# A hybrid encoder on one Trainium2 core: k's first four heads are turned by VectorE and DRAM instead of TensorE, and the opening and the layer border are put in another order

## The chip, the cores and the metric

The program runs on one core of one Trainium2 chip. The metric is the device time of one execution in microseconds (us). It is given as the median of the runs shown, and it stands beside one execution that was taken with a profile. The core has TensorE (PE in the profile, with its weight loads as PEld), VectorE (DVE), ScalarE (ACT), GpSimd (POOL) and SyncE (SP), which here issues transfers alone. Each engine takes its instructions in the order in which they stand in its own queue, and an instruction that waits holds up what stands behind it on that engine.

## The reference

Two layers (DEPTH = 2) over 256 tokens of width 1024, all in float32. A layer normalises its input, projects it by one wide matrix, runs two token mixers beside each other, gates and merges them and adds the result to its input. Cut to what matters here:

```python
for l in range(DEPTH):
    h = rmsnorm(x, norm_w[l])
    (q_a, k_a, v_a, ab_a, z_a, q_b, k_b, v_b, z_b, gate_a, gate_b) = split(h @ w_in[l])
    y_a = gated_delta_branch(q_a, k_a, v_a, ab_a, z_a, ...)   # short conv, silu, l2norm of q and k,
                                                              # chunked delta rule in both directions, 8 heads of 128
    y_b = diff_attention_branch(q_b, k_b, v_b, z_b, cos, sin, ...)   # partial rotary from positions
    merged = sigmoid(gate_a) * (y_a @ w_pa[l]) + sigmoid(gate_b) * (y_b @ w_pb[l])
    x = x + merged @ w_out[l]
return rmsnorm(x, final_norm_w)
```

For k the first branch needs both layouts: channels on the partitions (for the products of keys with keys and queries) and tokens on the partitions (`ktm`, for the update of the state), and the sum of squares of every token and head (`ssk`).

## The kernel before

**Products.** A float32 product is made of three products in a rounded format: each operand is split into a high part (ACT copies it into the rounded format) and a low part (DVE subtracts the high part from the original), and PE adds high by high, high by low and low by high. So every 512 KB piece of a weight matrix costs one transfer on SP's queue, one ACT cast (L290), one DVE subtraction (L292) and then the products. A weight matrix of 1024 rows and 512 columns comes in four such pieces, `kp` 0 to 3, each for two of the eight row blocks `kt`. The normalised input is turned by PE (`split_T`, L213) and split in the same way into `hT`, one half of it for `kt` 0 to 3 and one for 4 to 7, in two tiles `m` of 128 tokens.

**Order.** The scheduler of the language orders each engine's queue by a simulated time line and by priorities. The kernel's author steers it: `behind(ins)` puts an instruction after another in its engine's queue, and `mark` keeps the instructions that serve as such anchors.

**The opening.** The first norm's weights are one row. `norm_row` spreads it over the partitions: it lays the row into a tile of zeros and multiplies it by a matrix of ones below the diagonal, in two float32 products (L168). The positions come as one number per partition, in one small transfer on POOL's queue (L126). `prenorm` squares a token tile on ACT (L193), adds the sums on DVE (L188), takes the power on POOL (L189), multiplies on DVE (L203), and turns and splits both halves (L213, L219, L220). The first projection is v of the attention branch (`vb`, `proj_by_tile`, L364): it does all eight `kt` of token tile 0 and then all of token tile 1. Its first weight piece comes in halves (L276, L279, L281). Token tile 1 is loaded after weight piece 1, and its norm is made in the middle of tile 0's products. Later come `abp` (L563, sixteen small products) and then k.

**k, q and v of the first branch.** `proj_fm` leaves channels on the partitions. `evac_conv` then makes a head's short convolution: ACT scales (L610), DVE adds four taps (L614), ACT takes tanh (L620), DVE multiplies (L625). For k, `kq` holds the result, and for every pair of heads PE turns four blocks of 128 by 128 (L641) into a PSUM bank, ACT copies the bank to `ktm` (L643) and squares four blocks for `ssk` (L647). For v another way is in use already: DVE turns 32 by 32 blocks (`turn_squares`, L136), `bounce` writes them to DRAM (L141) and reads them back in four strided transfers (L143), all on POOL's queue, and `place_v` copies them on ACT later (L661). `log_decays` needs `ssk` of all heads, and the decays, `dsum` and `A` of the next stage hang on it.

**The border.** At the end of layer 0 the output projection's second half (`proj_by_tile`) is done tile by tile. After each tile its residual is added (L1207) and `prenorm` of the next layer runs, while `vb` of layer 1 begins with token tile 0. The turning of tile 1's first half stands ahead of the products of `kt` 6 of token tile 0.

Of the kernel before, what the change touches and what calls it, by code (L numbers as in the profile page):

```python
# [17 lines left out]
P = 128  # L18
# [31 lines left out]
def hybrid_encoder(  # L50
# [131 lines left out]
    def norm_factor(xt_, m, h, r, ss, halves_, after=None):  # L182


        for i in halves_:
            with behind(after):
                sq = mark["square", m, i] = square(xt_, m, h, ss, i)
        mark["sum"] = V.tensor_scalar(r, ss[:, 0:1], ss[:, 1:2], EPS, ALU.add, ALU.add).ins  # L188
        mark["pow"] = G.tensor_tensor(r, r, mhalf[:, :1], ALU.pow).ins  # L189
        return sq  # L190
# [4 lines left out]

    def normed(xt_, wb, m, nm, after=(None, None)):

        h, r, ss = norm_tiles(nm, m)
        sq = norm_factor(xt_, m, h, r, ss, range(2), after[0])
        for i in range(2):  # L200
            cs = slice(512 * i, 512 * i + 512)
            with behind(after[1]):
                hh = V.scalar_tensor_tensor(h[:, cs], xt_[i][:, m, :], r, wb[i],  # L203
                                            ALU.mult, ALU.mult).ins
        mark["norm", m] = sq, hh
        return h

    def split_T(dst, src, m, nm, bank=bank, w=None):


        pt = bank(f"pt_{nm}{m}")
        for j in range(4):
            tr = T.transpose(pt[:, j * P : (j + 1) * P], src[:, j, :], ident).ins  # L213
        mark["turn"] = tr
        ptv = pt.rearrange("p (j t) -> p j t", j=4)
        hi = dst[:, 0, :, m * P : (m + 1) * P]
        lo = dst[:, 1, :, m * P : (m + 1) * P]
        if w is None:
            a_ = S.copy(hi, ptv).ins  # L219
            mark["split"] = a_, V.tensor_tensor(lo, ptv, hi.bitcast(F32), ALU.subtract).ins  # L220
# [30 lines left out]
    def weights(w, c0, n, nm, homes=(None,) * 4, ahead=True, later=None, spare=(), held=None, turned=(), first=(),  # L251
                raws={}, halved={}):

# [3 lines left out]
        for kp in range(4):  # L257
            act, dve = (later or {}).get(kp, (None, None))
            act = mark[nm, act][0] if isinstance(act, int) else act
            with tc.high_priority(offset=HP) if ahead and (homes[kp] is None or kp in first) else nullcontext():  # L260
# [12 lines left out]
                if kp in halved:  # L273
                    for k in range(2):
                        rows = slice((2 * kp + k) * P, (2 * kp + k + 1) * P)
                        nc.sync.dma_start(out=raw[:, k, :n], in_=w[rows, c0 : c0 + n])  # L276
                        act, dve = halved[kp][k]
                        with behind(act):
                            high = S.copy(hi[:, k, :n], raw[:, k, :n]).ins  # L279
                        with behind(dve):  # L280
                            mark[nm, kp] = high, V.tensor_tensor(lo[:, k, :n], raw[:, k, :n],  # L281
                                                                 hi[:, k, :n].bitcast(F32), ALU.subtract).ins
                        yield 2 * kp + k, hi[:, k, :n], lo[:, k, :n]
# [38 lines left out]

    def proj_by_tile(act, w, c0, evac, nm, places, later=None, turn=None, spare=(), held=None, between=None,
                     cut=(), halved={}):

        accs = banks2(f"pp_{nm}")
        ws = []
        parts = weights(w, c0, 512, nm, places, ahead=False, later=later, spare=spare, held=held, halved=halved)  # L330
        if between is None:
            ws.extend(parts)
        for m in range(NM):
# [16 lines left out]
            for kt in range(KT):  # L350
                if len(ws) == kt:
                    if between and kt % 2 == 0:
                        between(kt)
                    ws.append(next(parts))
                if kt == 6 and turn and turn(m):
                    mark["proj"] = turn(m)
                if between and not m:
                    terms = [(kt - 1, 0, 0), (kt - 1, 1, 0), (kt, 0, 0), (kt, 1, 0),
                             (kt - 1, 0, 1), (kt, 0, 1)] if kt % 2 else []
                else:  # L360
                    terms = [(kt, 0, 0), (kt, 0, 1), (kt, 1, 0)]
                for n_, (k_, pa, pw) in enumerate(terms):
                    with behind(mark.get("proj")):
                        mark["proj"] = T.matmul(o, act[k_ // 4][:, pa, k_ % 4, ts_], ws[k_][1 + pw],  # L364
                                                start=k_ == 0 and n_ == 0,
                                                stop=kt == KT - 1 and n_ == len(terms) - 1).ins
            evac(m, o)
# [51 lines left out]
    def prenorm(m, xt_, wb_, l_, after=(None, None)):  # L419
        h = normed(xt_, wb_, m, f"n{l_}", after)  # L420
        for i in range(2):
            split_T(hT[i], heads4(h[:, 512 * i : 512 * i + 512]), m, f"h{l_}{i}", bank_c)
            mark["turn", m, i], mark["split", m, i] = mark["turn"], mark["split"]

    hT = pair("hT0")
    prenorm(0, xt, wb, 0)


    for l in range(DEPTH):
# [6 lines left out]
        def evac_v(i):  # L436
            def evac(m, ps):
# [8 lines left out]
                   for t_ in places2] + [places.pop(), *homes((("vtm", 1),), f"vb{l}1")]  # L446
        later, between, held, halved = {}, None, {}, {}
        if l == 0:
            halved[0] = (None, mark["norm", 0][1]), mark["split", 0, 0]

            def between(kt):
                if kt == 2:
                    later[1] = mark["split", 0, 1]
                elif kt == 4:
                    tokens(1)
                    prenorm(1, xt, wb, 0, mark["vb00", 1])
                    later[2] = mark["norm", 1]
                    mark["later"] = {0: mark["split", 1, 1]}
# [4 lines left out]
        for _ in proj_by_tile(hT, wl, C_VB, evac_v(0), f"vb{l}0", places, later=later,  # L463
                              spare=(1, 3) if l else (3,), held=held, halved=halved, between=between,
                              turn=lambda m: None if m or not l else mark["turn", 1, 0]):
            pass
        if l == 0:
# [3 lines left out]
            pos_f = const.tile([P, NM], F32, name="pos_f")  # L471
            with tc.issue_after(mark["split", 1, 1][1]):
                V.tensor_copy(pos_f, pos_i)
            freq = const.tile([P, RD], F32, name="freq")
# [128 lines left out]
        def conv(seg, c_base, slot, g):  # L603
            def evac_conv(acc, b0):
                vf = []
                for b in range(2):
# [12 lines left out]
                    th = ths[:, b, :]  # L619
                    S.activation(th, ca, AF.Tanh, scale=0.5)  # L620
                    if slot is None:
                        f_ = th.rearrange("p (m t) -> p m t", m=NM)
                    else:
                        f_ = kq[:, 4 * g + j4, :, slot, :]
                    mark["conv"] = V.scalar_tensor_tensor(  # L625
                        f_, th.rearrange("p (m t) -> p m t", m=NM), 1.0,
                        ca.rearrange("p (m t) -> p m t", m=NM), ALU.add, ALU.mult).ins
# [23 lines left out]

        loose = []

        def place_v(after):
# [633 lines left out]
```

## Time and profile before

| what | value |
|---|---|
| median of 3 runs | 751.92 us (751.69 to 752.0) |
| the profiled execution | 753.24 us, of which the profile's span is 751.5 us |
| granted TensorE clock in it | 0.997 |
| PE busy | 740.4 us |
| DVE busy | 588.9 us |
| ACT busy | 474.7 us |
| POOL busy | 143.1 us |
| bytes moved | 135.44 MB, mean 180 GB/s |

How to read it: the profiled execution is one run of its own and is 1.32 us longer than the median. A row of a time line gives start, duration, engine, source line, operation, output and inputs, and in square brackets how long the engine had been idle and what ended that. PE's matmuls are pipelined, so a matmul's duration is longer than its share of PE's time; the distance of two starts is the better price.

### The profile page before, as it was taken

The page shows a single profiled execution, that of the slowest core. Times are in us where ns is not written, and L with a number is a line of the kernel's source. Part 1 is how long each engine was busy: PE and PEld are TensorE (multiplying, and loading weights), DVE is VectorE, ACT ScalarE, POOL GpSimd, SP SyncE. Part 2 cuts the span into 40 slices and gives each one's busy share as a digit, 9 for nine tenths or more (in the row PEclk, how much of TensorE's full clock was granted, in tenths as well). Part 3 has the DMA queues.
Part 4 walks back from the last instruction along what each step waited for, and adds up shares of the span by engine and source line. Part 5 has one row for each costly group of instructions (what it writes and reads, how often), then busy time and mean ns, then how long its engine had stood idle before and what let it go on. Part 6 is the DMA issues. An engine that isn't in the chain of part 4 may idle for free.

```text
span 751.5 us, 13864 instructions
## 1 busy us (share of the span) xinstructions
PE 740.4 (99%) x5160; PEld 638.9 (85%) x5160; DVE 588.9 (78%) x1106; ACT 474.7 (63%) x1015; POOL 143.1 (19%) x221
## 2 busy tenths in 40 slices
PE   8999999999999999999999999999999999999996
PEld 5999889987888889888889889889778888998885
DVE  7786899999986865478667779999998769537782
ACT  6657665667877476645545577555777757566452
POOL 5100441111022440000010025202110425301000
PEclk9999999999999999999999999999999999999998
DMA  8752667776668462567674358768656847335641
GB/s 262 224 178 82 209 198 205 220 201 207 204 181 175 151 190 73 181 197 239 208 229 140 87 142 252 209 180 239 200 170 196 195 127 225 105 113 200 218 143 56
DMA packets 73474, 135.44 MB, mean 180 GB/s; under 512 B 12943, under 2 KB 13407, under 8 KB 73408
## 3 DMA queue, kind: packets, MB, share of 16 engines
q1 hardware_dynamic: 64606, 113.65, 50.2%
q0 software_dynamic: 7968, 19.35, 9.5%
q10 hardware_dynamic: 834, 1.58, 0.6%
q8 instruction: 40, 0.66, 0.4%
q14 instruction: 26, 0.21, 0.1%
HBM read 125.53 MB, written 9.01 MB: 179 GB/s over the span
## 4 chain that ended last, share of the span: by engine, by line
PE 92%; DVE 3%; issue 2%; DMA 1%; SPq 0%; POOL 0%; ACT 0%; POOLq 0%; DVEq 0%; ACTq 0%
PE pp_vb L364 5%; PE pp_qk L307 3%; PE pp_qk L308 3%; PE pp_qk L306 3%; PE sc L977 2%; PE pp_za L307 2%; PE pf_v L381 2%; PE pf_k L381 2%; PE pf_v L385 2%; PE pp_gb L307 2%; PE pp_gb L306 2%; PE pp_zb L306 2%; PE pf_k L383 2%; PE pf_k L385 2%; PE pf_v L383 2%
## 5 line engine op out<-in xcount | busy, mean ns | idle before, releaser
L307 PE MATMUL pp_qk<-lo_qk,hT 128*128 128x512 f32 x128 | 51.0, 398 | 0.8 <-DVE lo_qk L292 0.5
L308 PE MATMUL pp_qk<-hi_qk,hT 128*128 128x512 f32 x128 | 50.1, 391 | 0.0
L292 DVE TENSOR_TENSOR lo_qk<-raw_qk,hi_qk 128x1024 fp32r<-128x1024 f32 x32 | 39.6, 1239 | 9.6 <-ACT hi_qk L290 9.3
L306 PE MATMUL pp_qk<-hi_qk,hT 128*128 128x512 f32 x128 | 45.1, 393 | 0.0
L290 ACT CAST hi_qk<-raw_qk 128x1024 fp32r<-128x1024 f32 x28 | 29.4, 1049 | 24.0 <-PE pp_qk L308 11.7
L987 ACT ACTIVATE es<-sc,mx 128x256 f32<-128x256 f32 x64 | 29.6, 474 | 21.1 <-DVE mx L985 21.1
L383 PE MATMUL pf_q<-hT,hi_q 128*128 128x256 f32 x128 | 36.2, 286 | 0.0
L381 PE MATMUL pf_q<-hT,hi_q 128*128 128x256 f32 x128 | 36.1, 287 | 0.0
L292 DVE TENSOR_TENSOR lo_pb<-raw_pb,hi_pb 128x1024 fp32r<-128x1024 f32 x16 | 19.6, 1225 | 21.0 <-ACT hi_pb L290 20.9
L381 PE MATMUL pf_k<-hT,hi_k 128*128 128x256 f32 x128 | 36.0, 285 | 0.0
L381 PE MATMUL pf_v<-hT,hi_v 128*128 128x256 f32 x128 | 35.9, 285 | 0.0
L383 PE MATMUL pf_v<-hT,hi_v 128*128 128x256 f32 x128 | 35.8, 284 | 0.0
L383 PE MATMUL pf_k<-hT,hi_k 128*128 128x256 f32 x128 | 35.7, 283 | 0.0
L385 PE MATMUL pf_q<-hT,lo_q 128*128 128x256 f32 x128 | 34.9, 285 | 0.0
L385 PE MATMUL pf_v<-hT,lo_v 128*128 128x256 f32 x128 | 34.6, 288 | 0.0
L385 PE MATMUL pf_k<-hT,lo_k 128*128 128x256 f32 x128 | 34.3, 284 | 0.0
L614 DVE SCALAR_TENSOR_TENSOR cvq<-pf_q,cw,cvq 128x254 f32<-128x254 f32 (+1 forms) x64 | 29.9, 477 | 1.9 <-ACT cvq L610 1.4
L290 ACT CAST hi_pa<-raw_pa 128x1024 fp32r<-128x1024 f32 x16 | 16.8, 1052 | 22.3 <-PE pp_pa L308 16.1
L307 PEld LDWEIGHTS pp_qk<-lo_qk,hT 128*128 128x128 f32 x128 | 24.0, 188 | 7.9 <-DVE lo_qk L292 3.0
L614 DVE SCALAR_TENSOR_TENSOR cvv<-pf_v,cw,cvv 128x254 f32<-128x254 f32 (+1 forms) x64 | 30.1, 481 | 0.1
L614 DVE SCALAR_TENSOR_TENSOR cvk<-pf_k,cw,cvk 128x254 f32<-128x254 f32 (+1 forms) x64 | 28.5, 478 | 2.0 <-ACT cvk L610 1.3
L292 DVE TENSOR_TENSOR lo_pa<-raw_pa,hi_pa 128x1024 fp32r<-128x1024 f32 x16 | 19.6, 1225 | 11.1 <-ACT hi_pa L290 11.1
(393 smaller groups left out, 2538.2 us busy)
## 6 DMA issues: line engine op xcount, KB each, us to landing
raw_qk<-in_w_in_dram SPq DMA_DIRECT2D x32, 512.0 KB, 3.9
raw_k<-in_w_in_dram SPq DMA_DIRECT2D x16, 512.0 KB, 5.1
raw_q<-in_w_in_dram SPq DMA_DIRECT2D x16, 512.0 KB, 3.7
raw_v<-in_w_in_dram SPq DMA_DIRECT2D x16, 512.0 KB, 3.8
raw_zb<-in_w_in_dram SPq DMA_DIRECT2D x16, 512.0 KB, 3.9
raw_za<-in_w_in_dram SPq DMA_DIRECT2D x16, 512.0 KB, 3.8
raw_ga<-in_w_in_dram SPq DMA_DIRECT2D x16, 512.0 KB, 4.4
raw_pb<-in_w_pb_dram SPq DMA_DIRECT2D x16, 512.0 KB, 4.2
```

Of the source, the lines that this page charges most:

```text
L290: high = (V.tensor_copy if kp in turned else S.copy)(hi[:, :, :n], raw[:, :, :n]).ins
L292: mark[nm, kp] = high, V.tensor_tensor(lo[:, :, :n], raw[:, :, :n], hi[:, :, :n].bitcast(F32), ALU.subtract).ins
L306: T.matmul(o, act[kt // 4][:, 0, kt % 4, ts_], hi, start=kt == 0, stop=False)
L307: T.matmul(o, act[kt // 4][:, 0, kt % 4, ts_], lo, start=False, stop=False)
L308: mark["proj"] = T.matmul(o, act[kt // 4][:, 1, kt % 4, ts_], hi, start=False, stop=kt == KT - 1).ins
L364: mark["proj"] = T.matmul(o, act[k_ // 4][:, pa, k_ % 4, ts_], ws[k_][1 + pw], start=k_ == 0 and n_ == 0, stop=kt == KT - 1 and n_ == len( ...
L381: T.matmul(o, hi[:, cs], act[kt // 4][:, 0, kt % 4, :], start=first, stop=False, skip_group_check=True)
L383: T.matmul(o, hi[:, cs], act[kt // 4][:, 1, kt % 4, :], start=False, stop=False, skip_group_check=True)
L385: T.matmul(o, lo[:, cs], act[kt // 4][:, 0, kt % 4, :], start=False, stop=done, skip_group_check=True)
L614: V.scalar_tensor_tensor(ca[:, o0:o1], acc[:, b, o0 + sft : o1 + sft], cw[:, j, cb : cb + 1], ca[:, o0:o1], ALU.mult, ALU.add)
L977: mm = T.matmul(sp[n][:, qt * SEQ : (qt + 1) * SEQ], qkT[h // 4][rows, 0, h % 4, qt * P : (qt + 1) * P], qkT[h // 4][rows, 1, h % 4, :], s ...
L987: S.activation(es[:, n, qt, :], spv[:, qt, :], AF.Exp, bias=mx[:, n, qt : qt + 1], accum_out=s_all[:, h, n, qt : qt + 1])
```

## The change

Four things are changed together.

1. For k's heads 0 to 3 (`g == 0`), in both layers, PE's turning, ACT's copy out of PSUM and the squares from PSUM go. In their place stand DVE's block transposes, the way through DRAM on POOL's queue, and `place_k`, which copies and squares on ACT from SBUF, after the tanh of heads 6 and 7.
2. The opening is rebuilt. Token tile 1 is loaded ahead of weight piece 1. The products of the first projection go piece by piece over both token tiles, and the pins are others. In `norm_row` the second half of the row is multiplied in the rounded format in two parts.
3. At the border one low part (token tile 0, second half) is made after tile 1's sum, tile 1 is turned ahead of `kt` 7 instead of `kt` 6, and weight piece 3's low part is no longer held behind tile 1's sum.
4. The positions come as one row of 256 numbers on ACT's queue, are made floats on POOL and put on the partitions by two small PE products.

```diff
-    pos_i = const.tile([P, NM], I32, name="pos_i")
-    with nc.allow_non_contiguous_dma(reason="one position per partition"):
-        G.dma_start(out=pos_i, in_=positions.rearrange("o (m p) -> p (o m)", p=P))
+    pos_i = work.tile([1, SEQ], I32, tag="conv", name="pos_i", bufs=2)
+    pos_r = work.tile([1, SEQ], F32, tag="conv", name="pos_r", bufs=2)
...
     def norm_row(w_row, nm):
-        row = work.tile([P, DM], F32, tag="w4c", name=f"wr_{nm}", bufs=4)
+        row = work.tile([P, 512], F32, tag="w2c", name=f"wr_{nm}", bufs=3)
+        hl = work.tile([P, 2, 512], F32R, tag="w4c", name=f"wl_{nm}", bufs=4)
         w1 = work.tile([1, DM], F32, tag="w4c", name=f"w1_{nm}", bufs=4)
+        one = work.tile([P, P], F32R, tag="cwr", name=f"one_{nm}", bufs=1)
         nc.scalar.dma_start(out=w1, in_=w_row.unsqueeze(0))
+        nc.scalar.dma_start(out=pos_i, in_=positions)
         V.memset(row, 0.0)
+        V.memset(one.bitcast(F32), 1.0)
+        V.memset(hl.bitcast(F32), 0.0)
...
-        for i in range(2):
-            V.tensor_copy(row[0:1, 512 * i : 512 * i + 512], w1[:, 512 * i : 512 * i + 512])
-            mm = T.matmul(wb[i], tri[:, 0, :], row[:, 512 * i : 512 * i + 512], start=True, stop=True)
+        V.tensor_copy(row[0:1], w1[:, :512])
+        V.tensor_copy(hl[0:1, 0], w1[:, 512:])
+        V.tensor_tensor(hl[0:1, 1], w1[:, 512:], hl[0:1, 0].bitcast(F32), ALU.subtract)
+        for i in range(3):
+            mm = T.matmul(wb[i > 0], one if i else tri[:, 0, :], hl[:, i - 1] if i else row,
+                          start=i < 2, stop=i != 1)
...
@@ normed: a low part that was put off is made behind the sum of tile 1
+        while m and rest:
+            with behind(mark["sum"]):
+                rest.pop()()
+            mark["split", 0, 1] = mark["split"]
...
@@ prenorm
-            split_T(hT[i], heads4(h[:, 512 * i : 512 * i + 512]), m, f"h{l_}{i}", bank_c)
+            wait = l_ and not m and i
+            split_T(hT[i], heads4(h[:, 512 * i : 512 * i + 512]), m, f"h{l_}{i}", bank_c,
+                    late=rest if wait else None)
...
-    prenorm(0, xt, wb, 0)
+    G.tensor_copy(pos_r, pos_i)
+    pos_p = ps_p.tile([P, 512], F32, tag="p", name="pos")
+    for m in range(NM):
+        mm = T.matmul(pos_p[:, m : m + 1], pos_r[:, m * P : (m + 1) * P], ones[0:1, 0:1], start=True, stop=True)
+        tc.keep_in_program_order(mm)
+
+    def opening(w, evac, places):
+        accs = banks2("pp_vb00")
+        later, lows = {}, []
+        parts = weights(w, C_VB, 512, "vb00", places, ahead=False, later=later, spare=(3,), halved=(0,), late=lows)
+        ws = [next(parts), next(parts)]
+        tokens(1)
+        def products(m, kp, lower):
+            terms = [(2 * kp + k, pa, 0) for k in range(2) for pa in range(2)]
+            if lower:
+                terms = [(2 * kp + k, 0, 1) for k in range(2)]
+            for n_, (kt, pa, pw) in enumerate(terms):
+                with behind(mark["proj"]):
+                    mark["proj"] = T.matmul(accs[m], hT[kt // 4][:, pa, kt % 4, m * P : (m + 1) * P], ws[kt][1 + pw],
+                                            ...
+        def rows(m, i, h, **kw):
+            split_T(hT[i], heads4(h[:, 512 * i : 512 * i + 512]), m, f"h0{i}", bank_c, **kw)
+            mark["turn", m, i], mark["split", m, i] = mark["turn"], mark["split"]
+        h = normed(xt, wb, 0, "n0")
+        low = mark["norm", 0][1]
+        for high, lo, raw, hi in lows:
+            with behind(low):
+                low = V.tensor_tensor(lo, raw, hi, ALU.subtract).ins
+        rows(0, 0, h, after=(None, low))
+        made = norm_tiles("n0", 1)
+        norm_factor(xt, 1, *made, range(2), mark["split", 0, 0][0])
+        rows(0, 1, h, after=(mark["square", 1, 1], mark["sum"]))
+        mark["proj"] = mark["turn", 0, 1]
+        products(0, 0, False)
+        products(0, 0, True)
+        h = normed(xt, wb, 1, "n0", (None, mark["split", 0, 1][1]), made)
+        later[1] = mark["split", 0, 1][0], mark["norm", 1][1]
+        ws += [next(parts), next(parts)]
+        products(0, 1, False)
+        ws += [next(parts), next(parts)]
+        at = mark["proj"]
+        after = mark["vb00", 2]
+        for i in range(2):
+            rows(1, i, h, at=at, after=after)
+            at, after = mark["turn"], mark["split"]
+        mark["proj"] = at
+        products(0, 1, True)
+        later[3] = mark["split"]
+        ws += [next(parts), next(parts)]
+        for m, kp in ((0, 2), (1, 0), (1, 1), (1, 2), (0, 3), (1, 3)):
+            products(m, kp, False)
+            products(m, kp, True)
+            if kp == 3:
+                evac(m, accs[m])
+        mark["later"] = {0: mark["vb00", 3]}
...
@@ the layer loop, layer 1
-                     3: (mark["split", 0, 0][0], mark["sum"])}
+                     3: mark["split", 0, 0]}
-                              turn=lambda m: None if m or not l else mark["turn", 1, 0]):
-            pass
+                                   turn=lambda m: None if m else mark["turn", 1, 0], at=7):
+                pass
...
@@ evac_conv
-                if seg == "v":
-                    tb = squares(f"v{l}{g}{b0}")
-                    turn_squares(tb, ths.rearrange("p b (m t) -> p (b m) t", m=NM))
-                    bounce(tb, f"v{l}{g}{b0}")
+                if seg == "v" or g == 0:
+                    tb = squares(f"{seg}{l}{g}{b0}")
+                    turn_squares(tb, ths.rearrange("p b (m t) -> p (b m) t", m=NM) if seg == "v" else
+                                 kq[:, 4 * g + b0 : 4 * g + b0 + 2, :, slot, :].rearrange("p h m t -> p (h m) t"))
+                    bounce(tb, f"{seg}{l}{g}{b0}")
                     loose.append((tb, 4 * g + b0))
                     return
...
+        def place_k(after):
+            tb, h0 = loose.pop(0)
+            tbv = tb.rearrange("p i (b m) d -> p b m i d", m=NM)
+            for m in range(NM):
+                with behind(after):
+                    S.copy(ktm[:, m, h0 : h0 + 2, :].rearrange("p b (i d) -> p b i d", i=4), tbv[:, :, m])
+            for b in range(2):
+                for m in range(NM):
+                    with behind(after):
+                        S.activation(sqj[:, :P].rearrange("p (i d) -> p i d", i=4), tbv[:, b, m], AF.Square,
+                                     accum_out=ssk[:, m, h0 + b : h0 + b + 1])
...
         conv("k", C_KA, 0, 0)
         conv("k", C_KA, 0, 1)
+        for j4 in (2, 3):
+            place_k(mark["tanh", "k", 1, j4])
```

More of the change, by code (lines that the diff above doesn't have):

```diff
@@ L186, in norm_factor @@
             with behind(after):
-                sq = mark["square", m, i] = square(xt_, m, h, ss, i)
+                sq = mark["square", m, i] = after = square(xt_, m, h, ss, i)
         mark["sum"] = V.tensor_scalar(r, ss[:, 0:1], ss[:, 1:2], EPS, ALU.add, ALU.add).ins
@@ L194, in square, with normed @@
                             accum_out=ss[:, i : i + 1]).ins
-    def normed(xt_, wb, m, nm, after=(None, None)):
-        h, r, ss = norm_tiles(nm, m)
-        sq = norm_factor(xt_, m, h, r, ss, range(2), after[0])
+    rest = []
+    def normed(xt_, wb, m, nm, after=(None, None), made=None):
+        h, r, ss = made or norm_tiles(nm, m)
+        sq = mark["square", m, 1] if made else norm_factor(xt_, m, h, r, ss, range(2), after[0])
+        while m and rest:
+            with behind(mark["sum"]):
+                rest.pop()()
+            mark["split", 0, 1] = mark["split"]
         for i in range(2):
@@ L206, in normed, with split_T @@
         return h
-    def split_T(dst, src, m, nm, bank=bank, w=None):
+    def split_T(dst, src, m, nm, bank=bank, w=None, late=None, at=None, after=(None, None)):
         pt = bank(f"pt_{nm}{m}")
         for j in range(4):
-            tr = T.transpose(pt[:, j * P : (j + 1) * P], src[:, j, :], ident).ins
+            with behind(at):
+                tr = T.transpose(pt[:, j * P : (j + 1) * P], src[:, j, :], ident).ins
         mark["turn"] = tr
@@ L218, in split_T, with lower @@
         if w is None:
-            a_ = S.copy(hi, ptv).ins
-            mark["split"] = a_, V.tensor_tensor(lo, ptv, hi.bitcast(F32), ALU.subtract).ins
+            with behind(after[0]):
+                a_ = S.copy(hi, ptv).ins
+            def lower():
+                with behind(after[1]):
+                    mark["split"] = a_, V.tensor_tensor(lo, ptv, hi.bitcast(F32), ALU.subtract).ins
+            if late is None:
+                lower()
+            else:
+                late.append(lower)
         else:
@@ L276, in weights @@
                         nc.sync.dma_start(out=raw[:, k, :n], in_=w[rows, c0 : c0 + n])
[L277 to L282, printed above, removed]
+                        high = S.copy(hi[:, k, :n], raw[:, k, :n]).ins
+                        late.append((high, lo[:, k, :n], raw[:, k, :n], hi[:, k, :n].bitcast(F32)))
                         yield 2 * kp + k, hi[:, k, :n], lo[:, k, :n]
@@ L321, in homes, with proj_by_tile @@
                 yield t_[:, k]
-    def proj_by_tile(act, w, c0, evac, nm, places, later=None, turn=None, spare=(), held=None, between=None,
-                     cut=(), halved={}):
+    def proj_by_tile(act, w, c0, evac, nm, places, later=None, turn=None, spare=(), held=None, cut=(), at=6):
         accs = banks2(f"pp_{nm}")
[L329 to L332, printed above, removed]
+        ws = list(weights(w, c0, 512, nm, places, ahead=False, later=later, spare=spare, held=held))
         for m in range(NM):
@@ L350, in proj_by_tile @@
             for kt in range(KT):
[L351 to L355, printed above, removed]
-                    mark["proj"] = turn(m)
[L357 to L362, printed above, removed]
+                if kt == at and turn and turn(m):
+                    mark["proj"] = turn(m)
+                for n_, (pa, pw) in enumerate(((0, 0), (0, 1), (1, 0))):
                     with behind(mark.get("proj")):
-                        mark["proj"] = T.matmul(o, act[k_ // 4][:, pa, k_ % 4, ts_], ws[k_][1 + pw],
-                                                start=k_ == 0 and n_ == 0,
-                                                stop=kt == KT - 1 and n_ == len(terms) - 1).ins
+                        mark["proj"] = T.matmul(o, act[kt // 4][:, pa, kt % 4, ts_], ws[kt][1 + pw],
+                                                start=kt == 0 and n_ == 0, stop=kt == KT - 1 and n_ == 2).ins
             evac(m, o)
@@ L446, in hybrid_encoder @@
                    for t_ in places2] + [places.pop(), *homes((("vtm", 1),), f"vb{l}1")]
[L447 removed]
         if l == 0:
[L449 to L458, printed above, removed]
+            opening(wl, evac_v(0), places)
         else:
             later = {1: mark["norm", 0], 2: (mark["norm", 0][0], mark["split", 0, 0][1]),
[L461 removed]
+                     3: mark["split", 0, 0]}
             mark["later"] = {0: mark["norm", 1], 1: (mark["norm", 1][0], mark["split", 1, 1][1])}
[L463 to L466 removed]
+            for _ in proj_by_tile(hT, wl, C_VB, evac_v(0), f"vb{l}0", places, later=later, spare=(1, 3),
+                                  turn=lambda m: None if m else mark["turn", 1, 0], at=7):
+                pass
         if l == 0:
```

10 lines of the change are left out of this document (6 added, 4 removed).

## The prediction

> **What bounds the kernel now.** I read the page's busy times and chain first, then PE's waits, then the time lines of the three places that the diff touches.
>
> ```profile
> span 751.5 us, 13864 instructions
> ...
> PE 740.4 (99%) x5160; PEld 638.9 (85%) x5160; DVE 588.9 (78%) x1106; ACT 474.7 (63%) x1015; POOL 143.1 (19%) x221
> ...
> PE 92%; DVE 3%; issue 2%; DMA 1%; SPq 0%; POOL 0%; ACT 0%; POOLq 0%; DVEq 0%; ACTq 0%
> ```
>
> The second line says that PE is never without work for more than 11.1 us in sum, the third that 92% of the chain that ended last runs through PE. So a piece of PE work that leaves saves its own time, as long as nothing else is late in its place; work that is put on DVE, ACT or POOL costs nothing until PE waits for it. The list of PE's waits names where that is nearest (total, times, longest):
>
> ```profile
> PEld pp_qk L307 <- DVE lo_qk L292: 3.0, 6, 0.9
> ```
>
> **Part 1, k's first four heads.** What goes, on PE's time line, and the groups of the tile `ctk`:
>
> ```profile
> 60.36 0.38 PE L641 MATMUL ctk<-ident,kq 128*128 128x128 f32 x2
> 60.49 0.36 PE L381 MATMUL pf_q<-hT,hi_q 128*128 128x256 f32 x1
> 60.70 0.28 PE L383 MATMUL pf_q<-hT,hi_q 128*128 128x256 f32 x1
> 60.81 0.28 PE L385 MATMUL pf_q<-hT,lo_q 128*128 128x256 f32 x1
> ```
> ```profile
> L641 PE MATMUL ctk<-ident,kq x32: 270/272/273, 45.9 to 437.7; 128*128 128x128 f32 x32
> L647 ACT ACTIVATE sqj<-ctk x32: 268/283/303, 54.9 to 440.7; 128x128 f32<-128x128 f32 x32
> L647 ACT ACTIVATION_READ_ACCUMULATOR sqj<-ctk x32: 194/204/238, 55.1 to 440.9; 128x1 f32 x32
> L643 ACT COPY ktm<-ctk x8: 579/586/593, 54.4 to 438.8; 128x512 f32<-128x512 f32 x8
> ```
>
> Two turns and one product of pf_q take 60.70 - 60.36 = 0.34 us from start to start; a product alone takes 0.11 (60.70 to 60.81). Two turns cost PE 0.23. Half of the 32 turns go, eight pairs: 8 x 0.23 = **1.84 us off PE**. The duration of 0.27 would give more, but matmuls overlap, so I take the starts.
>
> The Trainium skill gives TensorE 390 ns for a 128 by 128 turn (of bf16) and advises TensorE for turns of that size where PSUM may hold the result ("VectorE: DVE Perf Modes", Rules for kernel authors); by that figure 6.2 us would go and the profiled time would end near 746.5. The rows above decide for 1.84, and the advice does not ask which engine is short.
>
> What comes instead, by the rows of v, which goes this way already:
>
> ```profile
> L143 POOL DMA_DIRECT2D tb_v<-bnc_v x32: 548/548/573, 145.7 to 555.8; - x32
> L661 ACT ACTIVATE vtm<-tb_v,nrm x32: 386/392/446, 156.8 to 559.8; 128x128 f32<-128x128 f32 x32
> L136 DVE STREAM_TRANSPOSE tb_v<-thv x8: 702/708/714, 140.9 to 549.4; 128x512 f32<-128x512 f32 x8
> ...
> DMA to landing us min/median/max: 2.1/3.2/5.1
> ```
> ```profile
> 141.91 0.58 POOL L141 DMA_DIRECT2D bnc_v<-tb_v  x1 [24.55 <-DVE stg L538]
> 145.70 2.20 POOL L143 DMA_DIRECT2D tb_v<-bnc_v  x4 [3.21 <-DMA bnc_v<-tb_v]
> ```
>
> DVE gains four block transposes of 0.71 us, 2.8 us in both layers. POOL gains four times five issues; its reads wait 3.21 us for the write, and behind them on POOL stands only the next pair's way, for the power of `log_decays` needs all of `ssk` anyway. ACT loses a copy of 0.59 per pair and gains two half as wide. The trace has no such copy from SBUF; it lies between 0.39 (L661, half its width) and 0.59 (L643, twice its width), so ACT pays 0.2 to 0.6 more per pair, 0.8 to 2.4 in all. The squares stay at 0.28 + 0.20 each. Does anything of this reach PE? In layer 0:
>
> ```profile
> 55.61 0.43 DVE L625 SCALAR_TENSOR_TENSOR kq<-thk,cvk 128x256 f32<-128x256 f32 x1 [0.48 <-ACT thk L620]
> ...
> 65.90 0.42 ACT L620 ACTIVATE thk<-cvk 128x256 f32<-128x256 f32 x1
> ...
> 67.05 1.05 ACT L290 CAST hi_q<-raw_q 128x1024 fp32r<-128x1024 f32 x1
> ...
> 68.13 1.23 DVE L292 TENSOR_TENSOR lo_q<-raw_q,hi_q 128x1024 fp32r<-128x1024 f32 x1 [0.79 <-ACT hi_q L290]
> ```
>
> Head 3 is finished at 56.04. From the start of a transpose to the last read's issue v takes 145.70 + 2.20 - 140.9 = 7.0 us, and 3.2 more to landing: the second pair is back at about 66.2. `place_k` stands for it behind the tanh of 65.90. So it comes just in time, 0.3 us late at the median and up to 2.2 at the slowest landing. DVE was idle for 0.48 before head 3, for a tanh that stood behind the copies and squares which now go; that pays a part of DVE's 0.71. I put 0.2 us on all of this together, near the lower end, because the wait that could hurt is short and `place_k` comes in six small pieces between which a cast can stand. The ends are 0 and 6 (rival B).
>
> **Part 2, the border.**
>
> ```profile
> 380.54 1.22 DVE L292 TENSOR_TENSOR wB_vb<-raw_vb,wB_vb 128x1024 fp32r<-128x1024 f32 x1
> 380.70 1.47 POOL L189 TENSOR_TENSOR xr_n<-xr_n,mhalf 128x1 f32<-128x1 f32 x1 [6.30 <-DVE xr_n L188]
> ...
> 380.95 1.52 PE L364 MATMUL pp_vb<-wvtm_vb,hT 128*128 128x512 f32 x6
> ...
> 382.21 1.42 DVE L203 SCALAR_TENSOR_TENSOR h_n<-xt,xr_n,wb_n 128x512 f32<-128x512 f32 x2 [0.45 <-POOL xr_n L189]
> ...
> 383.11 0.63 PE L213 MATMUL pt_h<-ident,h_n 128*128 128x128 f32 x4 [0.64 <-DVE h_n L203]
> ```
>
> Six products end at 380.95 + 6 x 0.23 = 382.33 (0.23 from the opening's rows below), and PE then stands until 383.11: 0.78 us. The three products of `kt` 6 that now come first are 0.69 us of work whose weights are split at 381.76. So the gap closes but for 0.1: **0.65 us off**. What is late next is the put-off low part: the third product of `kt` 4 needs it at 380.95 + 0.46 = 381.41. If DVE makes piece 3's low part (1.22) first from 380.54, and then this one (0.64), it comes at 382.40 and PE loses 1.0, so the ends are 0.78 off and 0.3 on.
>
> POOL's power took 1.47 us there and ended 0.41 after DVE's subtraction did. The Trainium skill has a reason ("SBUF — State Buffer", Who interferes with whom): a DVE instruction with two SBUF inputs and a GpSimd one that reads SBUF lock each other out. By that rule, with piece 3's low part made ahead of the sum, the power would not be held, and the gap would close whole, 0.1 us more; no row here shows that order.
>
> **Part 3, the opening and the positions.** Busy times of PE, PEld, DVE, ACT and POOL in the stretch, then single rows:
>
> ```profile
> 8.98:24.99 16.01, 14.99 (x74) 11.62 (x74) 13.39 (x31) 10.99 (x18) 8.88 (x11) 1.00 0.90 289
> ```
> ```profile
> 6.41 1.41 DVE L203 SCALAR_TENSOR_TENSOR h_n<-xt,xr_n,wb_n 128x512 f32<-128x512 f32 x2 [0.76 <-POOL xr_n L189]
> ...
> 7.83 0.62 ACT L279 CAST wA_vb<-raw_vb 128x512 fp32r<-128x512 f32 x1 [2.42 <-DMA raw_vb<-in_w_in_dram]
> ...
> 8.35 0.58 ACT L219 CAST hT<-pt_h 128x512 fp32r<-128x512 f32 x1
> ...
> 10.78 0.64 ACT L193 ACTIVATE h_n<-xt 128x512 f32<-128x512 f32 x1
> ...
> 11.40 0.63 ACT L193 ACTIVATE h_n<-xt 128x512 f32<-128x512 f32 x1
> ...
> 14.35 1.22 DVE L292 TENSOR_TENSOR wvtm_vb<-raw_vb,wvtm_vb 128x1024 fp32r<-128x1024 f32 x1
> ...
> 15.48 1.22 DVE L292 TENSOR_TENSOR wB_vb<-raw_vb,wB_vb 128x1024 fp32r<-128x1024 f32 x1
> ...
> 16.19 1.54 PE L364 MATMUL pp_vb<-wB_vb,hT 128*128 128x512 f32 x6
> 16.62 1.28 DVE L220 TENSOR_TENSOR hT<-pt_h,hT 128x512 fp32r<-128x512 f32 x2
> 17.57 1.52 PE L364 MATMUL pp_vb<-wA_vb,hT 128*128 128x512 f32 x6
> 23.16 1.98 PE L563 MATMUL abp<-hT,wabr 128*64 128x256 f32 x16
> ```
>
> Prices by distances of starts: a product 0.23 (six from 16.19 to 17.57), a half cast or copy on ACT 0.52, a square 0.62, a low part of a piece 1.13, one of a turned half 0.64. Of 16.01 us PE needs 48 x 0.23 = 11.0, eight turns at 0.115 = 0.9 and 1.8 for abp (23.16 to 24.99); 2.3 us are gaps, and that is all that can be won. Before, at 16.19, PE has 30 of the 48 products left. After, they again hang on DVE: ACT makes two casts and a copy from 7.83 on (to 9.39), tile 1's squares (10.63; its tokens come earlier, being ahead of a weight piece on SP), the second copy (11.15). DVE follows with its low part (11.8), tile 1's norm (1.41: 13.2), the low parts of pieces 1 and 2 (15.5), and that of tile 1's first half (16.1). Only then can PE go on to tile 1, and tile 0's pieces 0 to 2, 18 products, are done by then: 30 left at 16.1, where it was 16.19. What was won by the earlier tokens is used up by piece 1's low part, which is now pinned behind tile 1's norm. **0.1 us off**, between 2.3 off (no gaps) and 1.2 on (both squares in the way of what PE needs first).
>
> The rest of the opening is hidden: the weight row's products lie ahead of 6.41, where DVE waited for POOL's power and not for them; DVE has three more memsets and copies there, POOL a transfer less and one small cast more, ACT's queue a second issue behind the weight row's. If the positions landed late, PE's two position products would hold the first turns; the first transfers are back by then, so 0.
>
> **The sum.** The profiled execution took 753.24 us (span 751.5). 753.24 - 1.84 + 0.2 - 0.65 - 0.1 = 750.85. It was 1.32 above the median of 751.92, so the median after is **749.5 us**. About 0.2%, 1.5 us, is what a measurement of this kernel can tell from no change: 750.4 and 753.4 are the bounds.
>
> **Rivals.**
> A, the forecast, 749.5, chance 0.52; of it 0.06 lies above 750.4.
> O, the opening closes 1.4 of its 2.3 us of gaps as well: 748.1, chance 0.14. For it speaks that DVE's order there is only my reading.
> G, half given back: in the qk stage PE waits for DVE already (3.0 us in six waits). If DVE does not come earlier there with PE, each layer returns its 0.92: 751.3, chance 0.20. Against it: those waits are spread over the two layers and DVE's work there is itself released by PE.
> B, slower: the second pair is not back when `place_k` stands at the head of ACT's queue. Then the cast of 67.05 and DVE's low part of 68.13 come late, and PE's q products with them. It decides when the landing takes more than the 3.2 of v's median. At 5.1, ACT stands 2.2 us and has some of the 2.7 us of `place_k` (2 x 0.39 + 4 x 0.48) ahead of the cast as well: 3 us of PE per layer, 6 in all: 749.5 + 6 = 755.5, chance 0.14. The Trainium skill speaks for it ("VectorE: DVE Perf Modes", The three transpose paths): a plain strided transfer as a way of turning is 19 times slower than the crossbar's; v's strided reads land in 2.1 to 5.1 us, which does not show that.
>
> Faster: A 0.46 + O 0.14 = 0.60. Same: A 0.06 + G 0.20 = 0.26. Slower: 0.14. The range leaves B out and takes in O and G: 748.0 to 752.8. The forecast's own range is 748.8 to 750.4.
>
> **What would show it.** Right: 16 turns of L641's kind left instead of 32; no wait of PE behind hi_q or lo_q between the tanh of k's heads and the end of q; PE idle ahead of the border's first turn of tile 1 under 0.2 us; abp's start near 23.1. Wrong: a wait of ACT for the read-back of k with casts behind it (B); longer waits at lo_qk (G); abp starting over 1 us away from 23.16 (the opening).

## The result, and the profile after

| kernel | median, us | beside it, before | ratio, 95% interval |
|---|---|---|---|
| changed | 759.49 (4 runs, 757.12 to 760.36) | 751.96 | 1.0094 (1.0082 to 1.0105) |

The kernel became slower by 7.5 us by the medians, where 749.5 had been forecast and 748.0 to 752.8 was the range. The profiled execution took 760.36 us. Its busy times:

```profile
span 758.6 us, 13903 instructions
...
PE 741.0 (98%) x5148; PEld 639.4 (84%) x5148; DVE 591.9 (78%) x1113; ACT 477.4 (63%) x1019; POOL 153.8 (20%) x241
```

PE was without work for 11.1 us before and is for 17.6 us now. Its busy time did not fall although sixteen turns left, a point that comes back below. The groups of `ctk`, then those of `tb_k` (minimum, median, maximum in ns; first and last start in us):

```profile
L698 PE MATMUL ctk<-ident,kq x16: 270/272/273, 59.5 to 440.4; 128*128 128x128 f32 x16
```
```profile
L721 ACT ACTIVATE sqj<-tb_k x16: 296/311/318, 72.3 to 448.9; 128x128 f32<-128x128 f32 x16
...
L717 ACT COPY ktm<-tb_k x8: 396/410/422, 59.9 to 437.2; 128x256 f32<-128x256 f32 x8
L135 DVE STREAM_TRANSPOSE tb_k<-kq x4: 701/706/712, 48.5 to 427.2; 128x512 f32<-128x512 f32 x4
...
DMA to landing us min/median/max: 2.0/2.3/3.4
```

The operations have the sizes that were forecast: 16 turns left, 0.71 us for a block transpose, a copy of 0.41 between the bounds 0.39 and 0.59. The surprise is in the first starts of `tb_k`: the copies begin at 59.9, the squares of the same data at 72.3. ScalarE's time line, and the two steps that hang on it (`log_decays` on DVE and its first product on PE):

```profile
59.88 0.70 ACT L717 COPY ktm<-tb_k 128x256 f32<-128x256 f32 x2
...
64.75 0.72 ACT L717 COPY ktm<-tb_k 128x256 f32<-128x256 f32 x2
...
71.11 0.27 ACT L704 ACTIVATE sqj<-ctk 128x128 f32<-128x128 f32 x1
...
72.29 0.32 ACT L721 ACTIVATE sqj<-tb_k 128x128 f32<-128x128 f32 x1
...
76.89 0.19 ACT L721 ACTIVATION_READ_ACCUMULATOR sqj<-tb_k 128x1 f32 x1
...
77.28 0.17 DVE L741 TENSOR_SCALAR ge<-ssk 128x16 f32<-128x16 f32 x1
...
82.48 1.04 PE L759 MATMUL grps<-tri,glog 128*8 128x128 f32 x8
```

Before:

```profile
72.95 0.20 ACT L647 ACTIVATION_READ_ACCUMULATOR sqj<-ctk 128x1 f32 x1
...
73.33 0.17 DVE L671 TENSOR_SCALAR ge<-ssk 128x16 f32<-128x16 f32 x1
...
78.50 1.04 PE L689 MATMUL grps<-tri,glog 128*8 128x128 f32 x8
```

`ssk` is complete 4 us later (76.89 against 72.95), and so are `log_decays` and `grps`, though PE itself had come 1.6 to 1.7 us earlier to the q products and the qk stage. The list of waits (total, times, longest) shows what followed:

```profile
ACT vtm L731 <- DMA tb_v<-bnc_v: 9.2, 4, 3.7
...
PEld av L1085 <- ACT aT L1076: 4.3, 2, 2.3
...
PEld pp_qk L325 <- DVE lo_qk L310: 3.8, 4, 1.3
...
PEld pp_zb L325 <- DVE lo_zb L310: 3.2, 4, 1.3
```

The qk stages wait a little more for `lo_qk`. New is the stage of `zb` and `za`, where ACT stands for the read-back of v's fourth pair with the softmax behind it (after, then the same place before):

```profile
188.46 0.99 ACT L731 ACTIVATE vtm<-tb_v,nrm 128x128 f32<-128x128 f32 x3 [3.72 <-DMA tb_v<-bnc_v]
...
191.44 0.58 ACT L1076 COPY aT<-at 128x512 f32<-128x512 f32 x1
...
192.08 1.26 PE L1085 MATMUL av<-vb,aT 128*128 128x128 f32 x8 [1.86 <-ACT aT L1076]
```
```profile
191.21 0.61 ACT L1006 COPY aT<-at 128x512 f32<-128x512 f32 x1
191.67 1.31 ACT L661 ACTIVATE vtm<-tb_v,nrm 128x128 f32<-128x128 f32 x4
```

Before, `place_v` of that pair stood behind two casts of `hi_za` and behind `aT`, and waited for nothing. After, it stands ahead of `es`, `aT` and the casts.

By the starts of the same work in both traces, PE is ahead by 0.83 at the end of the opening and by 1.69 at the first qk product; 0.85 of that is gone at v's first product, 4.8 us go in layer 0's stage of `zb` and `za` (from 0.7 ahead to 4.1 behind), the border gains 0.58, layer 1's turns 0.9, and then its qk stage returns 1.3 and its `zb` and `za` stage loses 3.05. At the end PE is 7.1 behind.

Layer 0 lost 1.75 more than layer 1 in the same stage. The table of windows around the wait (window, length, PE busy and its instructions, granted clock, DMA share, GB/s) shows why:

```profile
190.00:191.00 1.00, 0.22 (x1) 1.00 0.00 0
191.00:192.00 1.00, 0.00 (x0) 1.00 0.00 0
...
193.00:194.00 1.00, 1.00 (x7) 0.50 0.00 0
194.00:195.00 1.00, 1.00 (x5) 0.50 0.03 8
195.00:196.00 1.00, 1.00 (x6) 0.50 0.67 82
196.00:197.00 1.00, 1.00 (x5) 0.80 0.92 326
```

After PE's stand of 1.86 us the granted clock is 0.50 for three windows and 0.80 for one: 3 x 0.5 + 0.2 = 1.7 us on top of the wait. This also explains a part of PE's busy time: slower matmuls count as busy. In layer 1 PE stood 1.62 us for `aT` at the same place, and the granted clock stayed at 1.00.

### The profile page after: what moved, and what is told of

It reads as the page before. It is cut to its first block, busy times and chain, and to the rows that moved or that the text cites. A ratio compares the mean times of both kernels' runs of the same rounds, so it can differ in the third digit from the quotient of the medians.

```text
span 758.6 us, 13903 instructions
## 1 busy us (share of the span) xinstructions
PE 741.0 (98%) x5148; PEld 639.4 (84%) x5148; DVE 591.9 (78%) x1113; ACT 477.4 (63%) x1019; POOL 153.8 (20%) x241
```

## Experiments

**Whose loss is it?** First k's turn was taken out of the changed kernel, then put alone into the kernel before.

```diff
-                if seg == "v" or g == 0:
+                if seg == "v":
...
-        for j4 in (2, 3):
-            place_k(mark["tanh", "k", 1, j4])
```

> The changed kernel with k's first four heads turned on PE as before; the rebuilt opening, the border's order and the positions as one row stay. Theory T: k's turn alone brings both losses (log_decays some 4 us later in each layer, and through the order that follows from it the fourth pair of v placed too early on ScalarE), while opening and border won 0.83 and 0.57 us. Then 751.96 - 0.83 - 0.57 = 750.6, with the zb and za stage of layer 0 at its former length (no +4.8) and no wait of ACT for v's read-back there. Rival U: the loss in the zb and za stages comes from the new opening or border, which shift what stands in the queues; then layer 0 still loses 4.8 and layer 1 3.05, and the time is 750.6 + 7.85 = 758.4.

Measured: 751.7 beside 752.18, ratio 0.9994 (0.9985 to 1.0003). PE's busy share has no gap in the `zb` and `za` stage. The waits for `lo_qk` and for v's read-back are short:

```profile
PEld pp_qk L325 <- DVE lo_qk L310: 2.4, 6, 0.6
...
ACT vtm L731 <- DMA tb_v<-bnc_v: 1.6, 2, 1.0
```

Rival U falls. The gain is 0.5 us instead of 1.4, and its interval includes no gain at all: the border won 0.56 in this trace too, the opening only 0.25.

The other way round, of the change only `place_k`, its two calls and the edit of `evac_conv` (as in the diff above) were put into the kernel before.

> The kernel before with k's block transposes, bounce and place_k alone; opening, border and positions as before. Theory T (both losses come with k's turn): 759.49 + 0.83 + 0.57 = 760.9, and in the trace the squares of tb_k end some 4 us later than those of ctk did and ACT waits over 3 us for v's read-back ahead of aT in the zb stage. Rival U (the zb and za stages lose by the opening or border): 751.96 - 1.8 for the turns + 0.85 + 1.3 given back in the qk stages = 752.3, and no such wait.

Measured: 762.16 beside 752.18, ratio 1.0131 (1.0117 to 1.0145), with `grps` at 83.26 and a wait of 3.9 us for v's read-back. Theory T holds: k's turn alone costs 10 us.

**Is the misplaced `place_v` the loss?** It was put one stage further back.

```diff
-            elif p == 1:
-                place_v(mark[f"zb{l}1", 1][0])
+            elif p == 2:
+                place_v(mark[f"za{l}0", 1][0])
```

> The changed kernel, with the placing of v's fourth pair put behind a product of the za stage's first half instead of one of the zb stage's second half. Theory T: what PE loses in the zb and za stages (4.8 and 3.05 us) is ACT standing for that pair's read-back ahead of es, aT and the casts of z; with the placing later ACT waits for none of it, and the time is 759.49 - 7.85 = 751.6 (at least 754 or below). Rival C: the transfers themselves are the loss (k's four more round trips share the DMA queues, or PE waits there for a weight piece); then moving the placing changes little and the time stays within 1 us of 759.5.

Measured: 755.21 beside 752.18, ratio 1.0042 (1.0029 to 1.0054). It is half right: 4.3 us below the changed kernel's median (3.9 by the ratios), not 7.85. ACT no longer waits there, but DVE's low parts still come late, and `grps` is as late as before the edit (83.33):

```profile
PEld pp_qk L325 <- DVE lo_qk L310: 4.5, 7, 1.3
PEld pp_zb L325 <- DVE lo_zb L310: 3.1, 4, 1.3
ACT vtm L731 <- DMA tb_v<-bnc_v: 1.7, 2, 1.0
```

So the wait was one of two consequences of something earlier.

**Why do the squares come so late?** First with priority:

```diff
         for j4 in (2, 3):
-            place_k(mark["tanh", "k", 1, j4])
+            with tc.high_priority(offset=HP):
+                place_k(mark["tanh", "k", 1, j4])
```

> The changed kernel, with place_k's copies and squares put first among ready work on ScalarE. Theory T: the squares then run with the copies near 65 to 68 instead of 72 to 77 us, log_decays starts as before (grps at 78.5 less what PE won), and each qk stage keeps the turns' gain: 0.85 + 1.3 = 2.1 us less, 757.4, if the order in the zb stage stays as it is; if that order follows from the late log_decays, it comes back too and the time is 759.5 - 2.1 - 7.85 = 749.5. Rival B2: placed first, the copies and squares stand ahead of q's casts and PE waits for hi_q or lo_q in q's first half, up to 3 us a layer: 759.5 + 6 - 2.1 = 763.

Measured: 758.87 beside 752.18, ratio 1.0092 (1.0078 to 1.0106), and the squares did not move:

```profile
71.06 0.27 ACT L704 ACTIVATE sqj<-ctk 128x128 f32<-128x128 f32 x1
...
72.24 0.32 ACT L721 ACTIVATE sqj<-tb_k 128x128 f32<-128x128 f32 x1
```

Neither outcome came: the order of ACT in this stage is that of the changed kernel. That was the hint. An order that priority doesn't change may be bound, and the two rows name what could bind it: all squares write the same scratch tile `sqj`, which nobody reads. `place_k` is written down after both calls of `conv` for k, so its squares are the later writers of `sqj` and must follow the last pair's, whose turns PE ends at 68.5. The copies go to separate places of `ktm` and were free to run. So the squares were written over `tb_k` itself, after the copies that read it:

```diff
-                        S.activation(sqj[:, :P].rearrange("p (i d) -> p i d", i=4), tbv[:, b, m], AF.Square,
+                        S.activation(tbv[:, b, m], tbv[:, b, m], AF.Square,
                                      accum_out=ssk[:, m, h0 + b : h0 + b + 1])
```

> The changed kernel, with place_k's eight squares of a layer's two pairs written over tb_k itself instead of into the scratch tile sqj. Theory S: in the changed kernel these squares share sqj with the squares of the last two pairs, which are written down earlier in the program, so they must follow the last of those (71.11 us) although their data was back by 60 and 65; that alone makes log_decays 4 us late, and the order of DVE and ScalarE that follows from it costs PE the rest. Then the squares run beside the copies, grps starts near 78.5 - 1.7 = 76.8, ACT does not wait for v's fourth pair, and the time is 759.5 - 2.15 (given back in the qk stages) - 7.85 (zb and za stages) = 749.5. Rival D: the way through DRAM itself is late or in the way (log_decays waits for the read-back, or v's transfers are slowed by k's); then grps stays near 82 and the time within 1.5 us of 759.5.

Measured: 749.03 beside 751.58, ratio 0.9963 (0.9951 to 0.9976). It beats both kernels. The squares run at once, and what hangs on them is early:

```profile
61.38 0.31 ACT L721 ACTIVATE tb_k<-tb_k 128x128 f32<-128x128 f32 x1
...
67.97 0.32 ACT L721 ACTIVATE tb_k<-tb_k 128x128 f32<-128x128 f32 x1
...
71.62 0.28 ACT L704 ACTIVATE sqj<-ctk 128x128 f32<-128x128 f32 x1
...
72.16 0.17 DVE L741 TENSOR_SCALAR ge<-ssk 128x16 f32<-128x16 f32 x1
...
77.33 1.04 PE L759 MATMUL grps<-tri,glog 128*8 128x128 f32 x8
```
```profile
PEld pp_qk L325 <- DVE lo_qk L310: 2.1, 6, 0.6
```

`place_v` of the fourth pair stands behind `aT` again (at 189.49, with no wait ahead of it), PE is ahead of the kernel before by 2.2 us through the whole of layer 0's `zb` and `za` stage, and by 3.8 at the end. (The execution of the kernel before whose trace is compared here took 753.24 us, longer than its medians of 751.58 to 752.18, so leads by the traces are larger than those by the medians.) Rival D falls.

**Are late squares enough without any transfer?** k is turned on PE as before; only the squares of its first two pairs are taken from `ktm` behind the last pair's.

```diff
                        hd = 4 * g + b0 + b
+                        if g == 0:
+                            kept.append((m, hd))
+                            continue
...
+        for m, hd in kept:
+            with behind(mark["tanh", "k", 1, 2 + hd // 2]):
+                S.activation(sqj[:, :P], ktm[:, m, hd, :], AF.Square, accum_out=ssk[:, m, hd : hd + 1])
```

> All of k turned on PE as in the kernel before, with the new opening, border and positions, and nothing of the way through DRAM; only the squares of the first two pairs are taken later, from ktm, behind the squares of the last pair, as they stand in the changed kernel. Theory S: late squares alone, without any transfer, bring both losses: 751.7 + 2.15 + 7.85 = 761.7, with grps near 83 and ACT waiting over 3 us for v's fourth pair ahead of aT. Rival D (the transfers): 751.7 plus at most 1, and v's fourth pair is placed as in the kernel before.

Measured: 759.44 beside 751.58, ratio 1.011 (1.0096 to 1.0124). Against the kernel that differs only in the squares' place (0.9994) that is 1.011 / 0.9994 = 1.2%, 8.7 us; squares in place against the changed kernel gave 1.0094 / 0.9963 = 1.3%, 9.9 us. The whole pattern is there without k's way through DRAM, if not in the same shares: 2.3 us less than forecast are lost, and PE loses 2.2 us in layer 0's stage of `zb` and `za` where it had lost 4.8 (1.7 of them by the half clock).

```profile
72.76 0.31 ACT L1113 ACTIVATE sqj<-ktm 128x128 f32<-128x128 f32 x1
...
78.99 0.17 DVE L745 TENSOR_SCALAR ge<-ssk 128x16 f32<-128x16 f32 x1
...
84.02 1.04 PE L763 MATMUL grps<-tri,glog 128*8 128x128 f32 x8
```
```profile
ACT vtm L735 <- DMA tb_v<-bnc_v: 6.8, 4, 2.9
PEld pp_qk L325 <- DVE lo_qk L310: 5.4, 7, 1.5
```

ACT's stand of 2.9 us is again at v's fourth pair, ahead of `es` and `aT` (189.33). The run also excludes that the late squares did harm by holding `tb_k`'s buffers, for here there are none.

**What is the turn worth by itself?** The kernel before with k's turn alone (as in the second experiment), its squares in place:

> The kernel before with k's turn alone, its squares in place; opening, border and positions as before. Theory S: the turns' 1.84 us come off and nothing is given back: 752.1 - 1.8 = 750.3, and the changed kernel with squares in place is 0.6 to 1.4 us below that by border and opening. Rival G (half given back in the qk stages even with early squares): 751.2 to 752.

Measured: 749.76 beside 751.58, ratio 0.9978 (0.9969 to 0.9987): 1.82 us, where 1.84 had been summed; the interval is 1.0 to 2.3 us. By the starts in the two traces PE takes 0.89 us less from `abp` to the first qk product in layer 0 and 0.95 less in layer 1, where all the turns of k lie: 1.84 in sum. Nothing is given back in the qk stages, whose waits are no longer than before (3.0 in six waits):

```profile
PEld pp_qk L307 <- DVE lo_qk L292: 2.1, 6, 0.6
```

The kernel with the other parts as well is 0.73 below it, but the two intervals overlap. Against the second experiment, from which it differs in the squares' output alone, the ratios give 1.0131 / 0.9978 = 1.5%, 11.5 us: the same edit, made a second time without the other parts, takes the loss away again.

**More of the same?** k's third pair by VectorE too, with squares in place and `place_v` of the fourth pair put back as above.

```diff
-                if seg == "v" or g == 0:
+                if seg == "v" or g == 0 or b0 == 0:
...
-        for j4 in (2, 3):
+        for j4 in (2, 3, 3):
```

> The changed kernel with squares in place, k's third pair (heads 4 and 5) turned by VectorE as well, so that 8 turns of L641's kind are left instead of 16, and v's fourth pair placed behind a product of the za stage's first half. Theory S with the prediction's price of 0.23 a pair of turns: four pairs more off PE, 0.9 us below the kernel with squares in place: 748.6. Rival K: the third pair's read-back comes after the last squares, log_decays is late by what it takes (a way of 10 us from about 62: 72, then eight copies and squares to 76), and the qk stages lose 1 to 2 us a layer: 751 to 753.

Measured: 756.72 beside 751.58, ratio 1.0078 (1.0064 to 1.0091); the five runs lie between 753.03 and 758.43, and the profiled one is the fastest of them, so its trace does not hold the whole loss. It shows the direction of K: the third pair's last square is read out at 73.16, `log_decays` starts at 73.39 instead of 72.16, `grps` 1.8 us later than with two pairs, and low parts of `zb` come late again.

```profile
71.46 0.72 ACT L717 COPY ktm<-tb_k 128x256 f32<-128x256 f32 x2
...
79.15 1.04 PE L759 MATMUL grps<-tri,glog 128*8 128x128 f32 x8
```
```profile
ACT vtm L731 <- DMA tb_v<-bnc_v: 4.2, 2, 2.2
PEld pp_zb L325 <- DVE lo_zb L310: 2.2, 4, 0.9
```

K's price (1 to 2 us a layer) was too small. What the slower runs add stays open: a lower clock alone does not explain it, for the run of 756.72 us had the granted clock of the profiled one, 0.998. Two things were edited at once, and what each costs was not told apart.

## Why the prediction was wrong

**The step that failed** is the sentence "The squares stay at 0.28 + 0.20 each" in part 1. Their duration is right (0.31 + 0.19); their place in ACT's queue was not asked for. The prediction followed each engine for room, took `place_k` to be six small pieces between which a cast can stand, and checked the read-back against the cast behind it. It named `log_decays` as the reader of all of `ssk`, but only to say what stands behind the reads on POOL; it did not ask when `ssk` would be complete, nor which earlier instructions the squares must follow. Both can be read without a run: the diff shows `sqj` as their output, and the prediction's own row of L647 shows the squares of `ctk` writing the same tile. With the last of those at 71.11, eight squares of about half a microsecond and the casts between them end near 77, against 73.0 before.

**The price of that step.** All that DVE, POOL and ACT took over was put at 0.2 us, between 0 and 6; the squares' place alone is 9.9 us (squares in place against the changed kernel). It has two consequences: PE's waits in the qk stages, and another order of DVE and ACT up to the `zb` and `za` stage. The misplaced fourth pair of v alone is 4.3 us of it by the medians, and in the profiled execution the half clock is 1.7 us. Three of the four signs of being right came all the same (16 turns left, no wait behind `hi_q` or `lo_q`, no gap at the border), and `abp` came within 1 us of its place: none of them watched the squares. Of the signs of being wrong only longer waits at `lo_qk` came, 3.8 us where it had been 3.0.

**Right:** PE's turns at 0.23 a pair: 1.82 us measured for the sum of 1.84. That the medians agree with it to 0.02 is luck, with an interval from 1.0 to 2.3 us; the starts of PE's work in that run's trace give it without luck. The estimate by the Trainium skill's 390 ns a turn (of bf16; "VectorE: DVE Perf Modes", The three transpose paths) would have been 6.2 us, which that interval excludes. The border: 0.65 forecast, 0.58 seen in the trace, with no gap left ahead of tile 1's turns:

```profile
386.61 0.85 PE L369 MATMUL pp_vb<-wB_vb,hT 128*128 128x512 f32 x3
387.30 0.60 PE L227 MATMUL pt_h<-ident,h_n 128*128 128x128 f32 x4
```

DVE makes piece 3's low part ahead of tile 1's sum there, and POOL's power took 0.56 us (at 385.01) where it had taken 1.47, as part 2 supposed for that order.

With squares in place 749.03 us were measured where 749.5 had been forecast for the whole change, so the other terms held in their sum. How much of it border and opening bring is not shown by the times: alone they gave 0.9994 (0.9985 to 1.0003).

**The opening:** 0.1 was forecast. `abp` starts at 22.34 after, 0.83 earlier, but the kernels with the same new opening start it between 21.97 and 23.20, and those with the old one between 22.55 and 23.16. A single trace can't size this part. In two of these traces (v's fourth pair placed later, 23.20, and late squares alone, 23.00) the granted clock was halved for a stretch of the opening, which the other traces with the same opening do not show.

**Rival B** (slower by the read-back of k) named the right side for the wrong reason. The read-back landed in 2.3 us at the median and both copies found it done; no wait of PE for `hi_q` or `lo_q` appears. The Trainium skill's trap of a strided transfer as a way of turning ("VectorE: DVE Perf Modes", The three transpose paths) was not felt in the two kernels that gained: their strided reads of k landed in 2.1 to 3.8 us and ACT never stood for them. No run compares them with the crossbar. **Rival G** forecast 1.84 given back in the qk stages, and 0.85 + 1.3 = 2.15 was; but it is no property of that stage, for with early squares it is gone.

**Open:** why a late `log_decays` puts v's fourth pair earlier in ACT's order was not shown. Where that pair's anchor was left as it was, the kernels with late squares, with and without transfers of k, place it ahead of `aT`; those with early squares place it behind.

## What to carry to other kernels

When work is moved to another engine, follow each of its outputs to the reader and ask when the last part of it is there, not only whether the engine has room. A scratch output that nobody reads is still an output: the instructions that wrote this tile kept their written order, so the moved ones, written down later, came after all earlier writers, and raising their priority changed nothing. Rows of one helper with a copy at 60 us and a square of the same data at 72 are how this looks in a trace, since an engine's own order shows as no wait.

## What the runs showed of the hardware

PE's stand of 1.86 us was followed by half the granted clock for 3.4 us (three windows at 0.50 and 0.4 us of a fourth); in the kernel before with k's turn a stand of 2.02 us was followed by the same, while with `place_k` first a stand of 1.78 us at the same place was not:

```profile
191.00:192.00 1.00, 0.00 (x0) 1.00 0.00 0
...
194.00:195.00 1.00, 1.00 (x9) 1.00 0.00 0
```

The Trainium skill lets the clock fall after an idle window of about 3.4 us that runs free of the program ("TensorE: Matmul & The Clock Gate", Part 1: The HAM clock gate). Here less than 2 us was enough, and the length of the slow stretch agrees with one such window. So the wait of 1.86 us cost 3.6 us, nearly twice its length.

The length of a single stand does not decide it. Stands of 1.62 and 1.78 us left the clock alone, while in the openings of two runs it was halved for as long as here after stands of 0.80 and 0.34 us (v's fourth pair placed later) and of 1.34 us (late squares alone). What decides it was not shown.
